# First projection after each of the last three norms, issued as two 128-token halves

## The chip, the cores and the metric

The kernel runs on one NeuronCore of a Trainium2 chip. The metric is device time in microseconds (us) of one execution, as a median over runs.

## What is computed

256 tokens of width 1024 go through two model blocks. The change touches only the second block, whose reference, cut down, is:

```python
def second_block(x, mem, ...):
    z = rmsnorm(h, mix_norm_g) @ w_in                 # h: 256 tokens x 1024
    y = concatenate([pool(z), rwkv7(z), diff_attention(z)])
    h = h + y @ w_out
    h = h + memory_cross_attention(rmsnorm(h, xa_norm_g), rmsnorm(mem, mem_norm_g),
                                   xa_wq, xa_wk, xa_wv, xa_wo, ...)
    h = h + conv_ffn(rmsnorm(h, ffn_norm_g), ffn_w_up, ffn_conv_w, ffn_conv_b, ffn_w_down)
    return h
```

So three norms stand ahead of three projections: the layer norm that ends the first model block (it feeds `w_in`), the norm ahead of `xa_wq`, and the norm ahead of `ffn_w_up`. All inputs are float32.

## The kernel before

**Split products.** Every large product is made of three: a float32 operand is split into `hi` (rounded, type fp32r) and `lo` (the rest), and hi·hi, lo·hi and hi·lo are summed in PSUM. `split` (line 198) does it with one ScalarE activation and one VectorE subtraction. Weights arrive as blocks of 128 x 1024 floats: `ws` loads one with a DMA into `raw` (3 buffers) and splits it into `hi` and `lo` (4 buffers each).

**Projections with the tokens in the free dimension.** `gemm_f` (line 225) multiplies one weight block (128 output features) with the activations `xh`, `xl`, which lie as 8 tiles of 128 features x 256 tokens. That is 3 x 8 = 24 matmuls, each with its own 128 x 128 stationary piece of the weights and 256 moving columns. Two such blocks, 48 matmuls, fill one PSUM tile `mm` of 128 x 512 floats. Pool `pm` has two `mm` tiles, used in turn.

**Output projections.** `rows_gemm` (lines 237 and 262) computes tokens x 1024 outputs into four accumulators: two token halves `tb`, each with two column halves. Its last 3 weight blocks (`TAIL`) are kept back and used for all of `tb=0` first, then for `tb=1`, so that the norm of the first 128 tokens can begin while the second half is still being multiplied.

**The norm in halves.** `done(tb)` runs for each half. For two of the three norms it is `add_turn`: VectorE adds the residual (line 474) and multiplies with the norm's gain (475); `turn` transposes four 128 x 128 pieces on TensorE into PSUM (line 280, tile `tp`), and `put` splits them to `xh`, `xl` (198). The per-token scale is not waited for: `row_norm` (ScalarE, 350) works out the mean square, and the scale is multiplied in behind the projection. For the layer norm of the first block, `layer_norm` (lines 399 to 438) does the same with more VectorE steps.

**Work that fills the layer norms.** Behind three layer norms, `rows_gemm` takes a `Fill`: 48 matmuls of the memory keys (line 94, tile `mk`) that are pinned in the order 30, 8, 10 around the transposes of `tb=1`:

```python
FILL = 30, 8, 10
...
            if fill is not None and tb == 1:
                self.turned, self.tgate = [], fill.part(FILL[0], ins)
            if done is not None:
                done(tb)
        if fill is not None:
            fill.rest()
```

`tgate` pins the transposes behind the first part; `turned` holds the last transpose of each column half, behind which the parts of 8 and 10 go; `pgate` pins the next projection behind the last transpose. These pins set only the order on TensorE. The rest of the order on each engine is settled by a scheduler before the program is compiled; each engine then runs its list strictly in order.

**The three places.** In this text place 1 is `columns` in `mixer` (weights `mix_f`, behind the layer norm with its `Fill` of memory keys), place 2 is `cross` (weights `xa_wq`, behind `add_turn`, without a fill), and place 3 is `ffn` (weights `ffn_up`, behind `add_turn`, without a fill).

Of the kernel before, what the change touches and what calls it, by code (L numbers as in the profile page):

```python
# [38 lines left out]
FILL = 30, 8, 10  # L39
# [6 lines left out]
class Parts:  # L46


    def __init__(self, parts):
        self.parts = parts  # L50
# [8 lines left out]
class Fill:  # L59
# [12 lines left out]
    def before(self, k):  # L72
        for f, i in self.at.get(k, ()):
            f(i)
# [32 lines left out]
    def rest(self):  # L107
        K, nc, h = self.K, self.K.nc, self.h
        self.part(FILL[1], K.turned[0])
        self.part(FILL[2], K.turned[1])  # L110
        p = self.p
        sq, k = (K.t2(n).rearrange("p (a b) -> p a b", a=2) for n in ("xsq", "mkey"))
        nc.scalar.activation(sq, p, AF.Square)
        for a in range(2):
            nc.scalar.activation(k[:, a], p[:, a], AF.Copy, scale=K.v("xk", a))

        def owed():
            nc.vector.tensor_add(sq[:, 0], sq[:, 0], sq[:, 1])
            ss = K.big("xss")
            for tb in range(2):  # L120
                nc.tensor.matmul(ss[:, tb:tb + 1], sq[:, 0, tb * 128:(tb + 1) * 128], K.ones[:, 0:1], start=True, stop=True)
            r = K.small(4, "kr")
            nc.vector.tensor_scalar(r[:, 2:4], ss[:, 0:2], 1.0 / 256, RMS_EPS, op0=OP.mult, op1=OP.add)
            K.power(r[:, 0:2], r[:, 2:4], 2)
            r = K.row_scale(r)
            nc.vector.tensor_mul(k, k, r[:, None, :].to_broadcast([128, 2, 256]))
            nc.sync.dma_start(K.kd[:, h], k.rearrange("p a b -> p (a b)"))

        K.owed = owed


class Kern:
# [992 lines left out]
    def mixer(self):  # L1125
        I = self.I
        xh, xl = self.xh, self.xl
        zp = self.page("zp")
        z = zp[:, 0:2048].rearrange("p (c t) -> p c t", c=8)

        A, T = self.page("rwA"), self.page("rwT")
        self.mk = self.load(A[:, 2560:3712].rearrange("p (m t) -> p m t", m=9), I["masks"])
        self.load(T[:, 2816:3328], I["lora"])
        self.load(T[:, 3584:4096].rearrange("p (c t) -> p c t", c=2), I["invcount"])
        self.rb = zp[:, 3840:4096]
        self.columns(z, 0, xh, xl)
        ypg = self.pages.tile([128, 2, 8, 256], F32R, name="ypg", tag="pg")
        yh, yl = (Parts([ypg[:, i, 0:4], ypg[:, i, 4:8]]) for i in range(2))
        self.weave((self.rwkv(z, A, T, yh, yl), 0, 0.8), (self.others(zp, A, T, xh, xl, yh, yl), 0, 1), (self.memory_kv(), MEM0, 0.8))
        accs = self.accs()  # L1140
        order = [4, 5, 6, 7, 0, 1, 2, 3]
        self.rows_gemm(accs, 8, lambda i: I["mix_out"][order[i]], lambda i: (yh, yl, order[i]), self.add_turn(accs, 1))

    def columns(self, dst, c0, xh, xl):
        for c in range(0, dst.shape[1], 2):
            p = self.mm().rearrange("p (a b) -> p a b", a=2)
            for a in range(2):
                hi, lo = self.ws(self.I["mix_f"][c0 + c + a], 1024)
                self.gemm_f(p[:, a, :], hi, lo, xh, xl, 8)
            if c0 + c < 4:  # L1150

                self.nc.scalar.activation(dst[:, c:c + 2], p, AF.Copy)
                if c == 2:
                    self.nc.scalar.activation(self.rb, self.row_scale(self.rn[:, 2:4]), AF.Copy)
                    for i in range(0, 4, 2):
                        self.nc.vector.tensor_mul(dst[:, i:i + 2], dst[:, i:i + 2], self.rb[:, None, :].to_broadcast([128, 2, 256]))
                    self.pay()
            else:
                self.nc.vector.tensor_mul(dst[:, c:c + 2], p, self.rb[:, None, :].to_broadcast([128, 2, 256]))
# [391 lines left out]
    def cross(self):  # L1551
        nc, I = self.nc, self.I
        kT, vt = self.mem
        xh, xl = self.xh, self.xl
        qp = self.page("qp")
        q = qp[:, 0:2048].rearrange("p (h a m) -> p h a m", h=4, a=2)
        PTs = qp[:, 2048:4096].rearrange("p (h k q) -> p h k q", h=4, k=2)
        norm = self.small(18, "xnorm")
        nc.vector.tensor_scalar(norm[:, 16:18], self.rn[:, 0:2], RMS_EPS, None, op0=OP.mult)
        for h in range(4):  # L1560
            p = self.mm().rearrange("p (a b) -> p a b", a=2)
            for a in range(2):
                hi, lo = self.ws(I["xa_wq"][h * 2 + a], 1024)
                self.gemm_f(p[:, a, :], hi, lo, xh, xl, 8)
            sq = self.t2("xsq").rearrange("p (a b) -> p a b", a=2)
            nc.scalar.activation(sq, p, AF.Square)
            for a in range(2):
                nc.scalar.activation(q[:, h, a], p[:, a], AF.Copy, scale=self.v("xq", a))
            nc.vector.tensor_add(sq[:, 0], sq[:, 0], sq[:, 1])
            ss = self.big("xss")  # L1570
            for tb in range(2):
                nc.tensor.matmul(ss[:, tb:tb + 1], sq[:, 0, tb * 128:(tb + 1) * 128], self.ones[:, 0:1], start=True, stop=True)
            r = norm[:, 2 * h:2 * h + 2]
            nc.vector.scalar_tensor_tensor(norm[:, 8 + 2 * h:10 + 2 * h], ss[:, 0:2], 1.0 / 256, norm[:, 16:18], op0=OP.mult, op1=OP.add)
            self.power(r, norm[:, 8 + 2 * h:10 + 2 * h], 2)
            nc.vector.tensor_scalar(r, r, 1.0 / 16, None, op0=OP.mult)
        opg = self.pages.tile([128, 2, 8, 256], F32R, name="xopg", tag="pg")
        oh, ol = (Parts([opg[:, i, 0:4], opg[:, i, 4:8]]) for i in range(2))
        for h in range(4):
            p = self.mm("s").rearrange("p (a b) -> p a b", a=2)  # L1580
            for tb in range(2):
                for a in range(2):
                    nc.tensor.matmul(p[:, tb], q[:, h, a, tb * 128:(tb + 1) * 128], kT[:, h, a], start=a == 0, stop=a == 1)
            self.softmax_t(p, norm[:, 2 * h:2 * h + 2], PTs[:, h])
            o = self.acc("o").rearrange("p (a b) -> p a b", a=2)
            for a in range(2):
                for mb in range(2):
                    c = h * 256 + a * 128
                    nc.tensor.matmul(o[:, a], vt[:, mb, c:c + 128], PTs[:, h, mb], start=mb == 0, stop=mb == 1)  # L1589
            self.split(oh.two(2 * h), ol.two(2 * h), o)  # L1590
        accs = self.accs()
        self.rows_gemm(accs, 8, lambda k: I["xa_wo"][k], lambda k: (oh, ol, k), self.add_turn(accs, 2))


    def ffn(self):
        nc, I = self.nc, self.I
        xh, xl = self.xh, self.xl
        w = I["ffn_up"]
        zs = []
        accs = None  # L1600
        gp = []
        for i in range(22):
            p = self.mm().rearrange("p (a b) -> p a b", a=2)
            for a in range(2):
                hi, lo = self.ws(w[a * 22 + i], 1024)
                self.gemm_f(p[:, a, :], hi, lo, xh, xl, 8)
            if i == 0:
                self.nc.scalar.activation(self.rb, self.row_scale(self.rn[:, 2:4]), AF.Copy)
            q = self.t2("q").rearrange("p (a b) -> p a b", a=2)
            nc.vector.tensor_mul(q, p, self.rb[:, None, :].to_broadcast([128, 2, 256]))  # L1610
            p = q
            c = self.t1("conv")
            cw = lambda j: self.v("cw", i * 3 + j)
            nc.scalar.activation(c, p[:, 0], AF.Identity, scale=cw(2), bias=self.v("cb", i))
            nc.vector.scalar_tensor_tensor(c[:, 1:], p[:, 0, :255], cw(1), c[:, 1:], op0=OP.mult, op1=OP.add)
            nc.vector.scalar_tensor_tensor(c[:, 2:], p[:, 0, :254], cw(0), c[:, 2:], op0=OP.mult, op1=OP.add)
            nc.scalar.activation(c, c, AF.Gelu)
            nc.vector.tensor_mul(c, c, p[:, 1])
            if i % 8 == 0:
                pg = self.pages.tile([128, 2, 8, 256], F32R, name="zf%d" % i, tag="pg")  # L1620
                gp.append([[pg[:, j, 0:4], pg[:, j, 4:8]] for j in range(2)])
            zh, zl = (Parts(gp[-1][j]) for j in range(2))
            self.split(zh[i % 8], zl[i % 8], c)
        zh, zl = (Parts([x for g in gp for x in g[j]]) for j in range(2))
        accs = self.accs()
# [168 lines left out]
```

## Time and profile before

| what | value |
|---|---|
| median of 3 runs | 2427.48 us (2427.36 to 2429.73) |
| the profiled execution: its own time | 2427.72 us |
| the profiled execution: span from first to last instruction | 2425.9 us |
| TensorE (PE) busy with matmuls | 2386.3 us, 98% of the span |
| TensorE busy with weight loads (PEld) | 2187.8 us, 90% |
| VectorE (DVE) busy | 1730.5 us, 71% |
| ScalarE (ACT) busy | 1185.7 us, 49% |
| GpSimd (POOL) busy | 50.9 us, 2% |
| mean granted TensorE clock, as a share of full speed | 0.996 |

TensorE's instructions overlap, so the busy time of one matmul is longer than the step from one to the next; the step is the start of the next row less the start of this one, over the number of matmuls. Idle time is shown in square brackets with the instruction that ended it.

### The profile page before, as it was taken

Reading aid. Unit: us, or ns where it says so; the run is one execution under the profiler, and the core shown is the slowest. Engines: PE = TensorE matmul, PEld = TensorE weight load, DVE = VectorE, ACT = ScalarE, POOL = GpSimd, SP = SyncE. Lnnn points to the kernel's source line nnn. Section 1 sums busy time; section 2 is a strip of 40 time slices with the busy share of each in tenths; the row PEclk is TensorE's granted clock in tenths of the full one; section 3 lists DMA queues with packets and bytes.
Section 4 is the critical chain, followed back from the end, with each engine's and each line's share of the span. In section 5 each row is a group of like instructions: output and inputs, shape, how many; then the busy total and the mean of one; then the engine's idle time right before and its main releaser. Section 6 shows DMA issues by size and latency. Waiting matters only on the chain.

```text
span 2425.9 us, 40782 instructions
## 1 busy us (share of the span) xinstructions
PE 2386.3 (98%) x16184; PEld 2187.8 (90%) x16184; DVE 1730.5 (71%) x3197; ACT 1185.7 (49%) x1620; POOL 50.9 (2%) x62
## 2 busy tenths in 40 slices
PE   8999999999999999989999999999999998999999
PEld 8888999999988888888999999998888887888997
DVE  8576699888755555676599888855555678765884
ACT  5454555444454444455555444444444455434553
POOL 0000000000000000000000000000000011000000
PEclk9999999999999999999999999999999999999999
DMA  6555554444555666634645444455666755133654
GB/s 229 186 210 203 192 185 174 154 160 158 173 190 192 217 205 220 204 116 158 222 168 189 158 156 159 165 185 192 196 227 200 248 168 167 62 110 122 195 183 156
DMA packets 121247, 433.82 MB, mean 179 GB/s; under 512 B 13920, under 2 KB 14560, under 8 KB 119648
## 3 DMA queue, kind: packets, MB, share of 16 engines
q1 hardware_dynamic: 120336, 430.95, 52.7%
q8 instruction: 127, 2.08, 0.3%
q14 instruction: 64, 0.52, 0.1%
q10 hardware_dynamic: 720, 0.26, 0.0%
HBM read 424.61 MB, written 6.55 MB: 178 GB/s over the span
## 4 chain that ended last, share of the span: by engine, by line
PE 95%; DVE 2%; ACT 1%; DMA 1%; issue 1%; POOL 0%; ACTq 0%; DVEq 0%
PE mm L225 45%; PE acc L237 37%; PE G L840 3%; PE acc L262 2%; PE mk L94 1%; PE scp L760 1%; PE y L670 1%; PE kq L225 1%; PE tp L280 1%; DVE lo L198 0%; PE c L225 0%; PE pXT L1453 0%; PE pX L1449 0%; ACT hi L198 0%; PE o L1589 0%
## 5 line engine op out<-in xcount | busy, mean ns | idle before, releaser
L198 DVE TENSOR_TENSOR lo<-raw,hi 128x1024 fp32r<-128x1024 f32 x752 | 917.0, 1223 | 462.3 <-ACT hi L198 460.5
L198 ACT ACTIVATE hi<-raw 128x1024 fp32r<-128x1024 f32 x752 | 791.4, 1056 | 757.0 <-PE acc L237 313.5
L225 PE MATMUL mm<-xh,hi 128*128 128x256 f32 x3056 | 445.8, 287 | 13.0 <-ACT hi L198 7.9
L225 PE MATMUL mm<-xl,hi 128*128 128x256 f32 x3056 | 436.1, 284 | 0.0
L225 PE MATMUL mm<-xh,lo 128*128 128x256 f32 x3056 | 433.0, 284 | 0.0
L225 PEld LDWEIGHTS mm<-xh,hi 128*128 128x128 f32 x3056 | 397.0, 192 | 15.7 <-ACT hi L198 7.9
L225 PEld LDWEIGHTS mm<-xl,hi 128*128 128x128 f32 x3056 | 396.9, 193 | 0.5 <-issue 0.5
L225 PEld LDWEIGHTS mm<-xh,lo 128*128 128x128 f32 x3056 | 396.0, 193 | 0.0
L237 PE MATMUL acc<-lo,xh 128*128 128x512 f32 x1112 | 345.4, 390 | 0.0
L237 PE MATMUL acc<-hi,xh 128*128 128x512 f32 x1112 | 344.9, 390 | 0.0
L237 PE MATMUL acc<-hi,xl 128*128 128x512 f32 x1112 | 344.5, 389 | 0.0
L237 PEld LDWEIGHTS acc<-hi,xl 128*128 128x128 f32 x1112 | 209.0, 188 | 43.6
L237 PEld LDWEIGHTS acc<-lo,xh 128*128 128x128 f32 x1112 | 209.2, 188 | 43.3
L237 PEld LDWEIGHTS acc<-hi,xh 128*128 128x128 f32 x1112 | 209.0, 188 | 43.3 <-issue 0.3
L819 ACT ACTIVATE H<-mm 128x512 f32<-128x512 f32 (+30 forms) x118 | 55.2, 468 | 193.2 <-PE mm L225 193.0
L198 DVE TENSOR_TENSOR xl<-H,xh 128x1024 fp32r<-128x1024 f32 x64 | 78.2, 1225 | 48.3 <-ACT xh L198 48.3
L198 ACT ACTIVATE xh<-H 128x1024 fp32r<-128x1024 f32 x64 | 67.5, 1058 | 57.5 <-PE acc L237 56.7
L840 PE MATMUL G<-h 128*128 128x128 f16 x1024 | 78.3, 220 | 0.0
L834 DVE TENSOR_TENSOR h<-iota,idxT 128x512 f16<-128x512 f16 x128 | 53.7, 421 | 26.8 <-PE G L840 26.6
L851 DVE SCALAR_TENSOR_TENSOR H<-G,H 128x512 f32<-128x512 f32 (+26 forms) x110 | 60.3, 551 | 13.8 <-ACT H L819 13.4
L840 PEld LDWEIGHTS <-h 128*128 128x128 f16 x1024 | 59.0, 97 | 4.8
L837 DVE TENSOR_TENSOR h<-h,idxT 128x512 f16<-128x512 f16 x128 | 53.6, 420 | 0.0
(519 smaller groups left out, 2150.8 us busy)
## 6 DMA issues: line engine op xcount, KB each, us to landing
raw<-in_peer_u_dram SPq DMA_DIRECT2D x256, 512.0 KB, 3.3
raw<-in_peer_v_dram SPq DMA_DIRECT2D x256, 512.0 KB, 4.2
raw<-in_ffn_up_dram SPq DMA_DIRECT2D x44, 512.0 KB, 3.6
raw<-in_peer_q_dram SPq DMA_DIRECT2D x32, 512.0 KB, 4.3
raw<-in_ffn_down_dram SPq DMA_DIRECT2D x22, 512.0 KB, 3.5
raw<-in_ret_g_dram SPq DMA_DIRECT2D x16, 512.0 KB, 4.0
raw<-in_ret_qk_dram SPq DMA_DIRECT2D x16, 512.0 KB, 3.7
raw<-in_ret_v_dram SPq DMA_DIRECT2D x16, 512.0 KB, 4.4
```

Source lines behind the costliest of these rows:

```text
L94: yield nc.tensor.matmul(self.p[:, a, :], self.W[:, 2 * a + w, k * 128:(k + 1) * 128], self.X[:, k, x], start=k == 0 and j == 0, stop=k == ...
L198: return self.nc.scalar.activation(hi, src, AF.Copy), self.nc.vector.tensor_sub(lo, src, hi.bitcast(F32))
L225: ins = self.nc.tensor.matmul(out, l[:, k * m:(k + 1) * m], r[k], start=k == 0 and j == 0, stop=k == nk - 1 and j == 2)
L237: ins = self.nc.tensor.matmul(o, l, r[:, c * n:(c + 1) * n], start=first and j == 0, stop=last and j == 2)
L262: last, ins = ins, self.nc.tensor.matmul(o, l[k][:, ts], r[:, c * 512:(c + 1) * 512], start=nk <= TAIL and i == 0 and j == 0, stop=i == le ...
L280: return self.nc.tensor.transpose(out, in_, self.ident)
L670: nc.tensor.matmul(y, AT[:, h, m, n * 128:(n + 1) * 128], vt[:, m, h * 512:(h + 1) * 512], start=m == 0, stop=m == 1)
L819: nc.scalar.activation(dst[:, :, tok:], p[:, :, tok:], AF.Gelu)
L834: nc.vector.tensor_tensor(o1, io, val[0], op=OP.is_equal)
L837: nc.vector.tensor_mul(o2, o2, val[2])
L840: nc.tensor.matmul(G[:, 4 * k + t, :], o1[:, t // 2, :, t % 2], o[:, t // 2, :, t % 2], start=i == 0, stop=i == 1)
L851: nc.vector.scalar_tensor_tensor(H[:, :n, ts], Gi[:, 64 * i:64 * i + n], 1 / GS, H[:, :n, ts], op0=OP.mult, op1=OP.mult)
```

## The change

A new class `Early` issues the first two weight blocks behind each of the three norms as half products: for each block 24 matmuls over the first 128 tokens, and after both blocks are done for those tokens, the same over the other 128. At places 2 and 3 it is given to `rows_gemm` as its `fill`: 30 half products stand ahead of the transposes of `tb=1`, and 18 more behind them (the 8 pinned behind the first column half, the 10 behind the second); the 48 of the second token half follow. At place 1, where the `Fill` of memory keys stays, all 96 come behind the transposes.

```diff
+class Early:
+    def __init__(self, K, w):
+        self.K, self.w = K, w
+        self.todo = None
+    def before(self, k):
+        pass
+    def products(self):
+        K = self.K
+        self.p = K.mm("early").rearrange("p (a b) -> p a b", a=2)
+        blocks = [K.ws(w, 1024) for w in self.w]
+        for tb in range(2):
+            ts = slice(tb * 128, (tb + 1) * 128)
+            for a, (hi, lo) in enumerate(blocks):
+                for j, (l, x) in enumerate(((hi, K.xh), (lo, K.xh), (hi, K.xl))):
+                    for k in range(8):
+                        yield K.nc.tensor.matmul(self.p[:, a, ts], l[:, k * 128:(k + 1) * 128], x[k][:, ts],
+                                                 start=k == 0 and j == 0, stop=k == 7 and j == 2)
+    def part(self, n, first):
+        if self.todo is None:
+            self.todo = self.products()
+        for i in range(n):
+            self.K.last = next(self.todo)
+            if i == 0:
+                self.K.after(self.K.last, first)
+        return self.K.last
+    def rest(self):
+        self.part(FILL[1], self.K.turned[0])
+        self.part(FILL[2], self.K.turned[1])
+        self.K.pgate = None
+    def all(self):
+        if self.todo is None:
+            self.part(48, self.K.turned[1])
+            self.K.pgate = None
+        for self.K.last in self.todo:
+            pass
+        return self.p
...
-        self.rows_gemm(accs, 8, lambda i: I["mix_out"][order[i]], lambda i: (yh, yl, order[i]), self.add_turn(accs, 1))
+        self.early = Early(self, I["xa_wq"][0:2])
+        self.rows_gemm(accs, 8, lambda i: I["mix_out"][order[i]], lambda i: (yh, yl, order[i]), self.add_turn(accs, 1), fill=self.early)
...
-            p = self.mm().rearrange("p (a b) -> p a b", a=2)
-            for a in range(2):
-                hi, lo = self.ws(self.I["mix_f"][c0 + c + a], 1024)
-                self.gemm_f(p[:, a, :], hi, lo, xh, xl, 8)
+            if c0 + c == 0:
+                p = Early(self, self.I["mix_f"][0:2]).all()
+            else:
+                p = self.mm().rearrange("p (a b) -> p a b", a=2)
+                for a in range(2):
+                    hi, lo = self.ws(self.I["mix_f"][c0 + c + a], 1024)
+                    self.gemm_f(p[:, a, :], hi, lo, xh, xl, 8)
...
-        self.rows_gemm(accs, 8, lambda k: I["xa_wo"][k], lambda k: (oh, ol, k), self.add_turn(accs, 2))
+        self.early = Early(self, (I["ffn_up"][0], I["ffn_up"][22]))
+        self.rows_gemm(accs, 8, lambda k: I["xa_wo"][k], lambda k: (oh, ol, k), self.add_turn(accs, 2), fill=self.early)
```

In `cross` (for `h == 0`) and `ffn` (for `i == 0`) the two `gemm_f` calls give way to `p = self.early.all()` in the same way. The changed file is 47 lines longer ahead of these functions, so line 280 of before is 327 after, 198 is 245, 225 is 272, 262 is 309, 350 is 397 and 361 is 408; the half products are line 151.

At place 3, TensorE's list before, from the last product of the output projection (`acc`) over the transposes (`tp`) to the projection (`mm`; `rb` carries the per-token scale):

```order
L262 MATMUL acc<-hi,xopg 128x512
L280 MATMUL tp<-ident,rms 128x128 x16
L225 MATMUL mm<-xh,hi 128x256 x8
L225 MATMUL mm<-xh,lo 128x256 x8
L225 MATMUL mm<-xl,hi 128x256 x4
L361 MATMUL rb<-ident,R 128x128
L225 MATMUL mm<-xl,hi 128x256 x4
```

The same place on the same engine in the changed kernel:

```order
L309 MATMUL acc<-hi,xopg 128x512
L327 MATMUL tp<-ident,rms 128x128 x8
L151 MATMUL early<-xh,hi 128x128 x8
L151 MATMUL early<-xh,lo 128x128 x8
L151 MATMUL early<-xl,hi 128x128 x8
L151 MATMUL early<-xh,hi 128x128 x6
L327 MATMUL tp<-ident,rms 128x128 x8
L151 MATMUL early<-xh,hi 128x128 x2
L408 MATMUL rb<-ident,R 128x128
L151 MATMUL early<-xh,lo 128x128 x8
L151 MATMUL early<-xl,hi 128x128 x8
```

The 16 transposes are now 8 and 8 with 30 half products between them; in all 96 matmuls of 128 columns take the place of 48 of 256. Place 2 has the same list, with one `acc` product still between the first two groups of four transposes.

ScalarE at place 3 before (`xh<-tp` copies a transposed half, `rms,ss<-h` is the mean square, `hi<-raw` splits a weight block):

```order
L198 ACTIVATE hi<-raw 128x1024 x5
L198 ACTIVATE xh<-tp 128x4x128 x2
L350 ACTIVATE rms,ss<-h 128x1024
L198 ACTIVATE xh<-tp 128x4x128 x2
L350 ACTIVATE rms,ss<-h 128x1024
L198 ACTIVATE hi<-raw 128x1024 x3
```

And after:

```order
L245 ACTIVATE hi<-raw 128x1024 x5
L245 ACTIVATE xh<-tp 128x4x128 x2
L397 ACTIVATE rms,ss<-h 128x1024
L245 ACTIVATE hi<-raw 128x1024 x2
L245 ACTIVATE xh<-tp 128x4x128 x2
L397 ACTIVATE rms,ss<-h 128x1024
L245 ACTIVATE hi<-raw 128x1024 x3
```

Two weight splits moved ahead of the copies of the second token half; VectorE's `lo` steps moved with them.

At place 1, TensorE's list before, with what each instruction waits for (a name is the engine whose semaphore is waited on):

```order
L94 MATMUL mk<-fill 128x256 x10
L225 MATMUL mm<-xh,hi 128x256 [waits DVE_49]
L225 MATMUL mm<-xh,hi 128x256 x3
L225 MATMUL mm<-xh,hi 128x256 [waits Activation_49]
L225 MATMUL mm<-xh,hi 128x256 x3
```

And after:

```order
L94 MATMUL mk<-fill 128x256 x10
L151 MATMUL early<-xh,hi 128x128 [waits DVE_49]
L151 MATMUL early<-xh,hi 128x128 x3
L151 MATMUL early<-xh,hi 128x128 [waits Activation_49]
L151 MATMUL early<-xh,hi 128x128 x3
```

Nothing moved here: the first half product stands where the first full product stood and also waits for VectorE.

## Rows read from the trace of the kernel before

**Rows 1.** The page: the chain that ended last, share of the span by engine.

```profile
PE 95%; DVE 2%; ACT 1%; DMA 1%; issue 1%; POOL 0%; ACTq 0%; DVEq 0%
```

**Rows 2.** Chain that ended last, in order: start us, us, what it ran.

```profile
1964.44 13.26 PE mm L225 x96
...
2237.60 0.22 PE rb L361 x2
...
2239.48 122.88 PE mm L225 x1024
2362.36 51.71 PE acc L237 x228
```

**Rows 3.** Timeline, place 2: start us, us, instruction, shapes, [idle before <-releaser].

```profile
2163.50 0.60 PE L280 MATMUL tp<-ident,rms 128*128 128x128 f32 x4
...
2164.13 1.27 ACT L198 ACTIVATE xh<-tp 128x512 fp32r<-128x512 f32 x2 [6.84 <-PE tp L280]
...
2164.17 1.04 PE L280 MATMUL tp<-ident,rms 128*128 128x128 f32 x8
...
2166.31 0.66 PE L280 MATMUL tp<-ident,rms 128*128 128x128 f32 x4 [1.11 <-DVE rms L475]
...
2166.97 1.42 PE L225 MATMUL mm<-xh,hi 128*128 128x256 f32 x8
...
2168.23 1.11 PE L225 MATMUL mm<-xh,lo 128*128 128x256 f32 x8
```

**Rows 4.** Timeline, place 3.

```profile
2231.64 1.47 PE L280 MATMUL tp<-ident,rms 128*128 128x128 f32 x12
...
2232.28 1.09 ACT L198 ACTIVATE xh<-tp 128x512 fp32r<-128x512 f32 x2 [6.13 <-PE tp L280]
...
2234.94 1.23 PE L225 MATMUL mm<-xh,hi 128*128 128x256 f32 x8 [0.97 <-ACT xh L198]
...
2236.00 1.12 PE L225 MATMUL mm<-xh,lo 128*128 128x256 f32 x8
...
2236.28 1.07 ACT L198 ACTIVATE hi<-raw 128x1024 fp32r<-128x1024 f32 x1
```

**Rows 5.** Timeline, place 1.

```profile
1957.63 1.18 ACT L198 ACTIVATE xh<-u 128x512 fp32r<-128x512 f32 x2
...
1963.70 0.69 DVE L198 TENSOR_TENSOR xl<-tp,xh 128x512 fp32r<-128x512 f32 x1
...
1964.44 1.27 PE L225 MATMUL mm<-xh,hi 128*128 128x256 f32 x8 [2.40 <-DVE xl L198]
```

**Rows 6.** Windows: stretch, its us, busy per engine, then granted PE clock, DMA share, GB/s.

```profile
1965.50:1968.90 3.40, 3.40 (x18) 3.40 (x17) 3.40 (x5) 0.04 (x1) 0.00 (x0) 0.50 0.51 164
...
2163.50:2167.00 3.50, 2.38 (x19) 1.84 (x17) 2.60 (x6) 2.72 (x5) 0.01 (x1) 1.00 0.00 0
...
2231.60:2235.00 3.40, 2.23 (x18) 1.72 (x16) 2.79 (x6) 2.72 (x6) 0.27 (x1) 1.00 0.00 0
```

**Rows 7.** Timeline of weight loads (PEld) around matmuls of one column, place 2.

```profile
2179.14 0.54 PEld L1572 LDWEIGHTS xss<-ones,xsq 128*128 128x128 f32 x4
2179.59 0.42 PEld L225 LDWEIGHTS mm<-xh,hi 128*128 128x128 f32 x3
```

**Rows 8.** Timeline, matmuls of 64 and 128 columns with float32 weights.

```profile
2043.04 1.97 PE L1405 MATMUL pv<-ident,W 128*128 128x64 f32 x16 [1.05 <-DVE W L1400]
2044.85 2.00 PE L1410 MATMUL pm<-rwab 128*128 128x128 f32 x16
```

**Rows 9.** Timeline, matmuls of 128 columns with float16 weights.

```profile
407.41 1.08 PE L840 MATMUL G<-h 128*128 128x128 f16 x16
408.30 0.84 PE L225 MATMUL mm<-xh,hi 128*128 128x256 f32 x5
```

**Rows 10.** Tiles: durations of weight loads in ns (min/median/max), first and last start.

```profile
L225 PEld LDWEIGHTS mm<-xh,hi x3056: 186/192/333, 7.9 to 2360.0; 128*128 128x128 f32 x191
...
L1405 PEld LDWEIGHTS pv<-ident,W x16: 186/192/192, 2043.0 to 2044.7; 128*128 128x128 f32 x16
```

More of the change, by code (lines that the diff above doesn't have):

```diff
@@ L1560, in cross @@
         for h in range(4):
[L1561 to L1564, printed above, removed]
+            if h == 0:
+                p = self.early.all()
+            else:
+                p = self.mm().rearrange("p (a b) -> p a b", a=2)
+                for a in range(2):
+                    hi, lo = self.ws(I["xa_wq"][h * 2 + a], 1024)
+                    self.gemm_f(p[:, a, :], hi, lo, xh, xl, 8)
             sq = self.t2("xsq").rearrange("p (a b) -> p a b", a=2)
@@ L1602, in ffn @@
         for i in range(22):
[L1603 to L1606, printed above, removed]
+            if i == 0:
+                p = self.early.all()
+            else:
+                p = self.mm().rearrange("p (a b) -> p a b", a=2)
+                for a in range(2):
+                    hi, lo = self.ws(w[a * 22 + i], 1024)
+                    self.gemm_f(p[:, a, :], hi, lo, xh, xl, 8)
             if i == 0:
```

## The prediction, made before the changed kernel was run

> **What bounds the kernel now.** I read the page first. The chain that ended last runs on TensorE for 95% of the span [rows 1], so whatever lengthens TensorE's list lengthens the run, unless it fills a wait. The chain in order of time then shows how fast that list runs: 1024 products of 256 columns in 122.88 us, or 0.120 us each, and 228 products of 512 columns in 51.71 us, or 0.2268 us each [rows 2]. Last I read the timelines of the three places for what TensorE waits for.
>
> At place 2 the transposes start at 2163.50 and the projection's second group of 8 starts at 2168.23 [rows 3]. In these 4.73 us stand 16 transposes, one product of 512 columns and 8 products of 256. A transpose takes 0.11 us (eight take 1.04 and four 0.60 [rows 3]), so 1.76 + 0.23 + 0.96 = 2.95 us is work and 1.78 us is waiting. At place 3 the same stretch is 2236.00 - 2231.64 = 4.36 us [rows 4], less 1.76 + 0.96: 1.64 us of waiting. In both, TensorE waits for VectorE to make the second token half and for ScalarE to copy it. At place 1 it waits 2.40 us for a VectorE step, `xl<-tp` [rows 5], and then runs 3.4 us at a granted clock of 0.50, the 1.2 GHz level [rows 6].
>
> **What the change removes.** At places 2 and 3 the first half products need only the first 128 tokens. At place 3 eight transposes end at 2231.64 + 0.88 = 2232.52; ScalarE's two copies run from 2232.28 for 1.09 us [rows 4], so the first is done at about 2232.82 and the second at 2233.37. Half products 1 to 4 read the first and wait 0.33 us; 5 to 8 wait 0.10 us more. The second token half's transposes then stand 30 half products later, when their inputs have long been ready. So 0.43 us of waiting stays of 1.64: 1.21 us is gained. At place 2 the same working, with transposes done at 2163.50 + 0.88 + 0.23 = 2164.61 and copies from 2164.13 for 1.27 us [rows 3], leaves 0.37 of 1.78: 1.41 us is gained.
>
> At place 1 I count no gain. The copies `xh` of the first 128 tokens begin at 1957.63 and take 1.18 us [rows 5], so these tokens were there long before TensorE stopped waiting at 1964.44. The wait is for a buffer: the new tile `early` comes from the same pool of two `mm` tiles as before, one of them holds the transposes that the VectorE step at 1963.70 reads, the other the memory keys. The order shows the same wait on VectorE at the first half product.
>
> **What it adds.** At each place 48 products of 256 columns (48 x 0.120 = 5.76 us) become 96 of 128 columns. Arithmetic does not grow, but the number of weight loads doubles, since every half product loads its own 128 x 128 stationary piece. No row shows an fp32r product of 128 columns, so its step is bounded. From below: 256 columns fewer save 0.2268 - 0.120 = 0.107 us [rows 2], so 128 fewer save 0.053 and a half product would take 0.067 us if the load stayed hidden. From above, with nothing saved, 0.120 us.
>
> The nearest rows speak for the upper end. Four matmuls of a single column each, with float32 weights, start their loads at 2179.14, and the load after them starts at 2179.59 [rows 7]: 0.1125 us per load with next to no columns to stream. Sixteen of 64 columns take 2044.85 - 2043.04 = 1.81 us, 0.113 us each [rows 8]. These are two-pass float32 products, but the load itself is alike: 192 ns median for `W` and 192 ns for the fp32r `hi` [rows 10]. So a load of 128 x 128 four-byte weights can follow another only after 0.11 us; under 256 columns (0.120) it is just hidden, under 128 it is the bound. Against this stand the float16 products of 128 columns: 16 from 407.41 to 408.30, 0.0556 us each [rows 9]. Their weights have two bytes, so I take the four-byte rows: 0.112 us.
>
> The Trainium skill, "TensorE: Matmul & The Clock Gate", has rules on either side. Its "Back-to-back issue gap" gives columns/2.4 + 2.5 ns, which is 56 ns here and fits the float16 rows; its "LDWEIGHTS" gives 128/1.2 = 107 ns for a load, and "Weight-path perf modes" says that fast loading does not hold for FP32, which fits the one-column rows. By the first rule a place would cost 96 x 0.056 - 5.76 = -0.4 us, by the second about +4.5 us.
>
> With 0.112, a place costs 96 x 0.112 - 5.76 = 10.75 - 5.76 = +4.99 us. This lies on TensorE's own list, with nothing beside it to hide it.
>
> **What is moved.** ScalarE does two weight splits of 1.07 us [rows 4] ahead of the second half's copies, which puts these back by some 2.1 us. They have cover: the transposes that these copies read come 30 half products (3.4 us) later than the first ones, and 18 more (2.0 us) stand between them and the first product that needs the copies. Without it the two splits would show as up to 2.1 us at either place. The blocks' buffers come free later, the first after 72 half products, the second after 96; two more blocks are split by then, 5.76 us of work for TensorE, against a split that takes 1.07 us on ScalarE and a like step on VectorE. At place 1 the load of the eighth `mix_f` block goes behind nine small loads in SP's queue; five blocks of 2.88 us lie between the freeing of its buffer and its use, so I cost it at nothing. The `rb` products (0.22 us each [rows 2]) stay as they are.
>
> **The sum.** 3 x 4.99 - 1.21 - 1.41 = +12.35 us. The profiled execution took 2427.72 us, 0.24 above the median of the three runs and inside their spread. 2427.72 + 12.35 = 2440.1; I say 2440.0 us, 0.5% slower. A measurement of this kernel can tell about 0.2%, 4.9 us, from no change.
>
> **Rivals.**
> - *Columns set the step after all.* fp32r loads hide as the float16 ones do. For it: rows 9, and that a load overlaps the matmul ahead. Against it: rows 7 and 8. At 0.056 us: 3 x (5.38 - 5.76) - 2.62 = -3.8 us, 2424; at 0.067 us: 3 x 0.67 - 2.62 = -0.6 us, 2427. This is the case on the other side: the change breaks even where 3 x (96p - 5.76) = 2.62, at p = 0.069 us, and is slower by over 0.2% from 0.086 us. The Trainium skill's same section also gives 81 ns for sustained pairs of load and matmul of 128 columns; that would be +3.4 us, 2431. Chance of this case 0.10.
> - *The clock falls too.* Half products leave the array idle for half of the time, and after a 2.40 us wait at place 1 the granted clock fell to 0.50 for 3.4 us [rows 5, 6]. At places 2 and 3, where TensorE is busy 2.38 of 3.50 and 2.23 of 3.40 us, it stayed at 1.00 [rows 6]. The change shortens these waits, which speaks against it. One such fall at half rate costs 1.7 us: at both places 2443.5, and more if it lasts through all half products. Chance 0.05.
> - *The narrow product leaves the fast form.* A true float32 product of 128 columns takes 0.22 us (`rb` [rows 2]). If 128 columns of fp32r ran so, a place costs 96 x 0.22 - 5.76 = 15.4 us, in all 2471. Nothing in the trace speaks for it. Chance 0.05.
> - *Place 1 gains as well*, if its wait is for the second token half and not for the tile: up to 2.40 us less, 2437.7. The order speaks against it. It lies inside the forecast's own range.
>
> **How the numbers follow.** The forecast (step near 0.11 us) has 0.80. Its own range: with 0.120 us and one fall of the clock, 3 x 5.76 - 2.62 + 1.7 = +16.4, 2444; with half of place 1's cost taken up later by waits of VectorE and the remaining waits gone too (0.8 us), 12.35 - 2.5 - 0.8 = +9.0, 2437. Down to 2434 it takes in steps around 0.09 us between the cases. So 2434 to 2445. Faster by over 0.2% needs a step under 0.053 us: 0.02. Within 0.2%: the rest of the first rival, 0.08. Slower: 0.90.
>
> **What would show it.** Right: rows of `early` with 8 matmuls starting every 0.9 us and loads every 0.11; at place 3 the first half products near 2232.9, at place 1 still near 1964.4 and behind `xl`; each place's 96 over some 10.8 us; no idle ahead of the second transposes. Wrong: groups of 8 every 0.45 to 0.55 us (the first rival), every 1.7 us (the third), a granted clock of 0.50 at place 2 or 3, or ScalarE's moved splits ending a wait of TensorE.

## The result and the profile after

| kernel | median (range), runs | ratio to before, 95% interval |
|---|---|---|
| before | 2427.42 us (2425.99 to 2429.73), 6 runs | |
| changed | 2451.79 us (2448.96 to 2452.83), 6 runs | 1.0095 (1.0085 to 1.0105) |

The change costs 24.4 us, about twice the 12.35 us forecast; 2451.8 lies above the range of 2434 to 2445. The profiled execution spans 2450.6 us, 24.7 more than before. It is one of four executions at 2451.2 to 2452.8 us with a mean granted clock of 0.991; the other two took 2449.0 and 2449.7 at 0.993.

The page of the changed kernel, first its busy time by engine, then the chain that ended last (in rows 1 PE had 95%):

```profile
PE 2413.3 (98%) x16328; PEld 2214.3 (90%) x16328; DVE 1731.6 (71%) x3197; ACT 1185.9 (48%) x1620; POOL 51.9 (2%) x62
...
PE 96%; DVE 2%; ACT 1%; DMA 1%; issue 1%; POOL 0%; ACTq 0%; DVEq 0%
```

TensorE is busy 27 us longer, and the engines other than TensorE hardly changed. So the question is where on TensorE's list the time went. The timeline of PE at place 1 answers to [rows 5]:

```profile
1963.94 1.25 PE L151 MATMUL early<-xh,hi 128*128 128x128 f32 x8 [2.42 <-DVE xl L245]
1964.98 1.91 PE L151 MATMUL early<-xh,lo 128*128 128x128 f32 x8
1966.69 1.91 PE L151 MATMUL early<-xl,hi 128*128 128x128 f32 x8
...
1983.76 2.02 PE L272 MATMUL mm<-xh,hi 128*128 128x256 f32 x8
...
1988.84 1.11 PE L272 MATMUL mm<-xh,hi 128*128 128x256 f32 x8
...
1991.71 0.61 PE L408 MATMUL rb<-ident,R 128*128 128x128 f32 x4
```

The wait for `xl` is the same as before (2.42 against 2.40 us), as forecast. But from the second group on, eight half products take 1.71 us, 0.2135 us each and not 0.112, and the first full-width products behind them are slow as well. Only from 1988.84 do eight full-width products take 0.95 us. The windows (stretch, its us, busy per engine, granted clock, DMA share, GB/s) say why; they answer to [rows 6]:

```profile
1965.20:1989.00 23.80, 23.80 (x114) 23.80 (x115) 8.93 (x12) 4.79 (x7) 3.26 (x5) 0.51 0.48 154
...
2040.30:2047.00 6.70, 6.17 (x17) 5.07 (x18) 6.19 (x15) 2.71 (x6) 3.60 (x2) 0.52 0.43 131
2060.80:2064.10 3.30, 3.30 (x17) 3.24 (x16) 1.47 (x5) 1.21 (x4) 0.00 (x0) 0.55 0.76 215
2183.00:2197.00 14.00, 14.00 (x126) 14.00 (x126) 8.09 (x13) 8.99 (x15) 1.10 (x2) 1.00 0.45 150
2251.50:2266.00 14.50, 14.25 (x122) 13.76 (x122) 9.79 (x15) 8.14 (x12) 1.12 (x2) 1.00 0.34 110
```

For 23.8 us TensorE is busy without a gap and the granted clock is 0.51, the 1.2 GHz level. Before, the same wait cost 3.4 us at 0.50 [rows 6]. At places 2 and 3 (the last two lines) the clock stays at 1.00. The chain in order of time gives the size of each piece:

```profile
1963.94 20.02 PE early L151 x96
...
2041.92 7.79 PE acc L284 x24
...
2060.29 3.38 PE pm L1461 x16
```

The rows of the kernel before that these and the next readings are compared with, first from its timeline of PE, then from its chain (`acc`, `pm` and further on `pv` and `pM` are tiles of the stages behind place 1; the tile `pm` is not the pool `pm`):

```profile
1977.54 0.61 PE L361 MATMUL rb<-ident,R 128*128 128x128 f32 x4
...
2173.98 1.12 PE L225 MATMUL mm<-xh,lo 128*128 128x256 f32 x8
...
2242.20 1.12 PE L225 MATMUL mm<-xh,lo 128*128 128x256 f32 x8
...
2027.75 6.74 PE acc L237 x24
...
2045.01 1.85 PE pm L1410 x16
```

- **Place 1.** From the first product to the first `rb` it took 1991.71 - 1963.94 = 27.77 us; before, 1977.54 - 1964.44 = 13.10. That is +14.67 where +4.99 stood.
- **Behind place 1**, the 24 `acc` products took 7.79 us (6.74 in the chain before) and the 16 `pm` 3.38 (1.85): +1.05 and +1.53, in the windows with clocks of 0.52 and 0.55. Before, the clock was at 0.50 from 2023.50 to 2030.30, over the first of these `acc` products too, and at 1.00 over `pm`.
- **Places 2 and 3**, from the first transpose to the second group of the third block:

```profile
2180.55 0.60 PE L327 MATMUL tp<-ident,rms 128*128 128x128 f32 x4
...
2183.01 1.06 PE L151 MATMUL early<-xh,lo 128*128 128x128 f32 x8
2183.90 1.06 PE L151 MATMUL early<-xl,hi 128*128 128x128 f32 x8
...
2194.68 1.12 PE L272 MATMUL mm<-xh,lo 128*128 128x256 f32 x8
...
2252.46 1.03 PE L327 MATMUL tp<-ident,rms 128*128 128x128 f32 x8
2253.74 1.15 PE L151 MATMUL early<-xh,hi 128*128 128x128 f32 x8 [0.25 <-ACT xh L245]
...
2257.19 1.06 PE L327 MATMUL tp<-ident,rms 128*128 128x128 f32 x8
...
2266.85 1.12 PE L272 MATMUL mm<-xh,lo 128*128 128x256 f32 x8
```

Place 2: 14.13 us against 10.48 before (2163.50 to 2173.98), +3.65; forecast 4.99 - 1.41 = 3.58. Place 3: 14.39 against 10.56 (2231.64 to 2242.20), +3.83; forecast 3.78. Eight half products take 0.89 us, 0.111 to 0.112 each. The second token half's transposes (2257.19) wait for nothing, and ScalarE's moved splits end no wait of TensorE. The five terms add up to 14.67 + 1.05 + 1.53 + 3.65 + 3.83 = 24.73 us, and the spans differ by 24.7. That the two agree to the last digit is chance: the changed kernel begins place 1 0.50 us earlier (1963.94 against 1964.44), so about 0.5 us more lies in small pieces outside the five terms.

### The profile page after: what moved, and what is told of

Same layout as the page of the kernel before. It is cut to its first block, busy times and chain, and to the rows that moved or that the text cites. A ratio compares the mean times of both kernels' runs of the same rounds, so it can differ in the third digit from the quotient of the medians.

```text
span 2450.6 us, 41070 instructions
## 1 busy us (share of the span) xinstructions
PE 2413.3 (98%) x16328; PEld 2214.3 (90%) x16328; DVE 1731.6 (71%) x3197; ACT 1185.9 (48%) x1620; POOL 51.9 (2%) x62
## 4 chain that ended last, share of the span: by engine, by line
PE 96%; DVE 2%; ACT 1%; DMA 1%; issue 1%; POOL 0%; ACTq 0%; DVEq 0%
PE mm L272 44%; PE acc L284 37%; PE G L887 2%; PE acc L309 2%; PE early L151 2%; PE mk L94 1%; PE scp L807 1%; PE tp L327 1%; PE y L717 1%; PE kq L272 1%; DVE lo L245 0%; PE c L272 0%; PE pXT L1504 0%; PE pX L1500 0%; PE o L1643 0%
## 5 line engine op out<-in xcount | busy, mean ns | idle before, releaser
L272 PE MATMUL mm<-xh,hi 128*128 128x256 f32 x3008 | 439.7, 287 | 9.1 <-ACT hi L245 7.8
L272 PE MATMUL mm<-xl,hi 128*128 128x256 f32 x3008 | 429.0, 284 | 0.0
L272 PE MATMUL mm<-xh,lo 128*128 128x256 f32 x3008 | 426.5, 284 | 0.0
L272 PEld LDWEIGHTS mm<-xh,hi 128*128 128x128 f32 x3008 | 391.5, 192 | 11.1 <-ACT hi L245 7.8
L272 PEld LDWEIGHTS mm<-xl,hi 128*128 128x128 f32 x3008 | 390.5, 193 | 0.5 <-issue 0.5
L272 PEld LDWEIGHTS mm<-xh,lo 128*128 128x128 f32 x3008 | 389.9, 193 | 0.0
```

The source lines that it names most:

```text
L272: ins = self.nc.tensor.matmul(out, l[:, k * m:(k + 1) * m], r[k], start=k == 0 and j == 0, stop=k == nk - 1 and j == 2)
```

## The experiments

Theory: two separate things cost time, the load-bound step of 0.112 us at all three places, and at place 1 a granted clock that falls behind the wait and does not come back while half products run. Rivals: the half products are slow at place 1 for another reason (their loads, their buffers, their number), or the places disturb each other. Differences are to the runs of the kernel before on the same chip: 2428.05 us (19 runs) for the first four kernels, 2427.93 (24 runs) for the next four and 2427.34 (21 runs) for the last three.

**1. Places 2 and 3 alone.** Against the changed kernel:

```diff
-            if c0 + c == 0:
-                p = Early(self, self.I["mix_f"][0:2]).all()
-            else:
...
+            p = self.mm().rearrange("p (a b) -> p a b", a=2)
```

> Half products at places 2 and 3 alone; place 1 as before. Theory (places 2 and 3 cost what was predicted, the surplus is place 1's clock): 96 half products a place at 0.112 us each, waits mostly gone, +3.65 and +3.83 us, so about +7.5 us, 2435, with a granted clock of 1.00 at both places. Rival (the half products cost more than was predicted everywhere): +12 us or more.

Measured 2435.41 us, ratio 1.0028 (1.0018 to 1.0037): +7.4, as expected. The terms of places 2 and 3 were right.

**2. Place 1 alone.** `fill=self.early` and the calls in `cross` and `ffn` taken back.

> Half products at place 1 alone. Theory (TensorE starts them at a granted clock of 0.50 after the 2.40 us wait and, as long as only half products run, the clock is not given back): some 23 us at 0.5, +14.7 us at the place, and up to 2.5 us more from falls of the clock further on, 2442 to 2445. Rival (the surplus comes from places 2 and 3 or from their sum): +5 us, 2432.

Measured 2444.50 us, ratio 1.0062 (1.0045 to 1.0078): +16.4, with a granted clock of 0.50 over 23.7 us:

```profile
1966.30:1990.00 23.70, 23.70 (x112) 23.70 (x112) 9.05 (x12) 4.79 (x7) 3.26 (x5) 0.50 0.48 153
```

With experiment 1 it makes 23.8 of the 24.4 us, so within their spread the places add up and do not disturb each other.

**3. The whole change, without the wait at place 1.** The last 24 products of the memory keys are issued once more into the same tile (their values don't change), and TensorE does them in place of waiting (`h == 3` is the `Fill` at place 1):

```diff
+        if h == 3:
+            for j, (w, x) in enumerate(((0, 0), (1, 0), (0, 1))):
+                for k in range(8):
+                    ins = nc.tensor.matmul(self.p[:, 1, :], self.W[:, 2 + w, k * 128:(k + 1) * 128], self.X[:, k, x],
+                                           start=k == 0 and j == 0, stop=k == 7 and j == 2)
+            K.pgate = K.turned[1] = ins
```

> The whole change, and 24 of the memory-key products of 256 columns are done once more (same operands, same result) in the wait of place 1, so that TensorE does not stand still for 2.40 us there. Theory: the clock stays at 1.00 through the half products, place 1 costs 0.5 us for what sticks out of the repeated products and 10.75 + 5.76 - 13.26 = 3.3 us, in all some +11 us, 2438. Rival (half products pull the clock down by themselves at this place): 0.5 again, +24 us or more, 2452.

Measured 2439.28 us, ratio 1.0042 (1.0026 to 1.0059): +11.2, where the changed kernel has +24.4, with 24 matmuls more. The window over its half products at place 1:

```profile
1964.60:1975.20 10.60, 10.60 (x97) 10.60 (x97) 8.04 (x12) 4.58 (x8) 3.17 (x5) 1.00 0.59 192
```

The same 96 half products, with the same operands, take 0.89 us per eight once no standstill is ahead of them. So without the wait the clock stays up at this place, and with the clock up the forecast's step holds.

**4. The same 24 products in the kernel before.**

> The kernel before with the same 24 repeated products in the wait of place 1. Theory: the 3.4 us at a granted clock of 0.50 behind this wait go away; they cost 1.7 us, the repeated products stick out by 0.5 us, so -1.2 us, 2426. Rival (the clock falls for another reason than the wait): +0.5 to +2.9 us.

Measured 2428.58 us, ratio 1.0001 (0.9991 to 1.0010): the expected gain of 1.2 us did not show, though the interval does not rule it out. Three windows of the profiled execution, at place 1 and at two falls of the clock further on (the first of them is in the kernel before as well):

```profile
1961.30:1975.70 14.40, 14.40 (x123) 14.40 (x122) 12.10 (x18) 9.40 (x14) 2.00 (x4) 1.00 0.49 166
2022.80:2029.50 6.70, 4.60 (x13) 3.83 (x14) 6.63 (x16) 2.31 (x5) 2.09 (x1) 0.51 0.63 157
2043.30:2050.00 6.70, 6.70 (x30) 6.34 (x30) 4.25 (x8) 1.61 (x3) 0.00 (x0) 0.51 0.77 212
```

The clock stayed up at place 1 and `rb` came 1.84 us earlier (1975.70 against 1977.54), but in this execution (2429.65 us) the clock fell over `pm` at 2043.30, where before it was at 1.00, and `pM` behind it is 1.46 us late (2048.15 against 2046.69). This is one of three executions at a mean granted clock of 0.996; the seven at 0.997 have a median of 2427.96 us, no clear gain either. So that fall is hardly the whole reason, and what else takes the gain is open.

**5. The same number of loads at place 1, at full width.** Place 1 alone again; both passes multiply all 256 tokens, so the 48 products are done twice:

```diff
-            ts = slice(tb * 128, (tb + 1) * 128)
+            ts = slice(0, 256)
```

> Place 1 alone with the same 96 products and 96 weight loads, but each over all 256 columns (everything is computed twice, the second time over the first). Theory (products of full width bring the clock back, half products do not): the clock is at 0.50 for 3.4 us as before, then 1.00, and 48 more products of 0.120 us cost +5.8 us, 2433, less than the half products with half the columns. Rival (it is the number of weight loads at this place): some 23 us at 0.50, +16 us, 2444.

Measured 2434.50 us, ratio 1.0027 (1.0016 to 1.0038): +6.6, where experiment 2 has +16.4, for twice the columns.

```profile
1965.40:1968.70 3.30, 3.30 (x18) 3.30 (x18) 3.30 (x5) 0.00 (x0) 0.00 (x0) 0.52 0.70 176
1968.90:1983.00 14.10, 14.10 (x120) 14.10 (x119) 6.39 (x9) 5.92 (x9) 3.26 (x5) 1.00 0.71 239
```

After 3.3 us the clock is back, as in [rows 6]. What the edit changes between the two kernels is the columns of each product alone, so the number of loads, the buffers and the order of the blocks are out as causes.

**6. Product series by themselves.** Ahead of `ffn`'s last stage, five series of fp32r products into a tile of their own (`dm`): 200 of 128 columns, 48 with 64 weight columns, 48 of 64, 48 of 192 and 48 of 256 columns.

> The kernel before with five series of fp32r matmuls ahead of the last projection (they compute nothing that is used): 200 with 128 x 128 weights and 128 columns, then 48 each with 128 x 64 weights and 128 columns, with 128 x 128 weights and 64, 192 and 256 columns. Theory (the load of four-byte weights sets the step): 0.112 us at 64, 128 and 192 columns alike, 0.120 at 256, and about 0.06 to 0.07 at 128 columns with half the weights; the clock stays at 1.00 through the 22 us of the first series. Rival (columns set it): 0.04, 0.067, 0.093 and 0.120 us, and the half weights change nothing.

One execution: 2471.59 us. The windows, for these matmuls alone (PE and PEld busy, then clock, DMA share, GB/s):

```profile
2362.00:2382.00 20.00, 20.00 (x181) 20.00 (x181) 1.00 0.06 24
2383.50:2386.10 2.60, 2.60 (x47) 2.60 (x45) 1.00 0.03 6
2386.40:2390.30 3.90, 3.90 (x38) 3.90 (x36) 1.00 0.00 0
2390.60:2392.40 1.80, 1.80 (x10) 1.80 (x10) 0.50 0.00 0
2397.40:2400.00 2.60, 2.60 (x25) 2.60 (x25) 1.00 0.00 0
2400.40:2405.80 5.40, 5.40 (x48) 5.40 (x47) 1.00 0.01 3
```

20.00 / 181 = 0.1105 us at 128 columns; with half as wide a stationary piece 2.60 / 47 = 0.055 us; 0.103 at 64 columns, 0.104 at 192, 0.1125 at 256 (a matmul cut by a window's edge counts whole, so the values of the short windows are some per cent low). The step follows the weight load and not the moving columns, up to 192 of them at least. And the clock: it stayed at 1.00 through 20 us of 128-column products, but fell to 0.50 at 2390.4, by the count of products inside the series of 64 columns, with TensorE busy all the time; it was back at 1.00 at 2397.4, within the series of 192 columns. The 2.6 us ahead of the 64-column series were the products with half as wide weights, so which of the two series brought the fall is not separated.

**7. A shorter wait at place 1, in the kernel before.** VectorE's step on the second 128 tokens that is needed only later (line 437; line 438 needs its result) is pinned behind the split of a weight block (`first`), which stands behind the copies, so that `xl` comes earlier:

```diff
-                    nc.vector.scalar_tensor_tensor(y[:, 1], y[:, 1], m, gb[:, 0], op0=OP.subtract, op1=OP.mult)
+                    a = nc.vector.scalar_tensor_tensor(y[:, 1], y[:, 1], m, gb[:, 0], op0=OP.subtract, op1=OP.mult)
+                    if first is not None:
+                        self.after(a, first)
```

> The kernel before, with the two VectorE steps of the last layer norm that are needed later (lines 437 and 438, 1.28 us each) pinned behind the copies that place 1 waits for. Theory: the wait of 2.40 us shrinks to some 0.5 us, and if it is short enough the clock does not fall: -1.9 us, or -3.5 us with the clock, 2424 to 2426. Rival (other work is late next, the split of the first weight block or the norm's scale): no change, or up to +2 us.

Measured 2428.49 us, ratio 0.9998 (0.9989 to 1.0007): no gain. The timeline shows the wait for `xl` down from 2.40 to 0.22 us and eight products in 0.96 us from the second group on, but two new waits for the norm's scale:

```profile
1962.62 1.21 PE L225 MATMUL mm<-xh,hi 128*128 128x256 f32 x8 [0.22 <-DVE xl L198]
...
1976.40 0.49 PE L361 MATMUL rb<-ident,R 128*128 128x128 f32 x2 [2.01 <-DVE R L360]
...
1977.09 1.20 PE L225 MATMUL mm<-xh,hi 128*128 128x256 f32 x8
1978.13 1.12 PE L225 MATMUL mm<-xh,lo 128*128 128x256 f32 x8
...
1982.38 0.68 PE L361 MATMUL rb<-ident,R 128*128 128x128 f32 x4 [1.24 <-DVE R L360]
```

The clock did not fall behind the wait of 2.01 us: the eight products from 1977.09 took 1.04 us. So a wait of about this length is not always followed by a fall.

**8. One block in halves, not two, at places 2 and 3.** 16 half products ahead of the second token half's transposes, 32 behind them; the second block in full width.

> Places 2 and 3 only, and there only the first block (24 products) in halves, 16 of them ahead of the transposes of the second token half; the second block in full width. Theory (a product that is split costs 2 x 0.112 - 0.120 = 0.104 us, and the filled waits give back 1.2 and 1.4 us): 48 x 0.104 - 2.6 = +2.4 us, 2430. Rival (the waits are worth more than the loads cost once fewer products are split): below the kernel before.

Measured 2431.36 us, ratio 1.0012 (1.0003 to 1.0022): +3.4, one more than expected and about half of experiment 1. A product split in two costs 2 x 0.112 - 0.120 = 0.104 us more, and the half that goes ahead fills at most 0.112 us of waiting. So a split wins next to nothing even where the half fills a wait, and here some of the halves fill none; splitting less only loses less.

**9. Experiment 7 with the scale applied one pair of blocks later.**

```diff
-            if c0 + c < 4:
+            if c0 + c < 6:
...
-                if c == 2:
+                if c == 4:
...
-                    for i in range(0, 4, 2):
+                    for i in range(0, 6, 2):
```

> The kernel before with VectorE's steps on the low halves pinned behind the copies, and the row scale rb of the first projection applied one pair of blocks later. Theory: the two rb waits of 2.01 and 1.24 us that ate the gain of the pinned copies are now behind work that TensorE has anyway, while the 2.4 us wait at place 1 stays gone and the clock stays at 1.00: 2 to 3.5 us less than the kernel before, 2424.5 to 2426. Rival: the first rb broadcast still comes too early for VectorE, or VectorE's work on what follows the projection starts later by what the scale was moved: no change, or up to 3 us more.

Measured 2429.56 us, ratio 1.0005 (0.9996 to 1.0014): no change, as the rival had it. The first `rb` still comes behind the fourth block, and waits; in the profiled execution the clock, at 1.00 through the first 96 products, falls there:

```profile
1977.42 0.49 PE L361 MATMUL rb<-ident,R 128*128 128x128 f32 x2 [1.82 <-DVE R L360]
...
1978.20:1981.60 3.40, 3.40 (x18) 3.40 (x18) 2.72 (x5) 0.56 (x1) 3.40 (x3) 0.51 1.00 389
```

Here a wait of 1.82 us for the same instruction is followed by a fall, where the 2.01 us of experiment 7 were not. Why, no run settles.

**10 and 11. The same products at place 1 in two orders.** Place 1 alone; one of the two blocks goes in halves, either the second or the first:

```diff
-        for tb in range(2):
-            ts = slice(tb * 128, (tb + 1) * 128)
-            for a, (hi, lo) in enumerate(blocks):
+        for a, ts in ((0, slice(0, 256)), (1, slice(0, 128)), (1, slice(128, 256))):   # experiment 10
+        for a, ts in ((0, slice(0, 128)), (0, slice(128, 256)), (1, slice(0, 256))):   # experiment 11
+            for hi, lo in (blocks[a],):
```

> Only place 1 changed: its first block in full width (24 products of 256 columns), then its second block in two halves (48 products of 128 columns). Theory (the clock that the wait takes away comes back behind full-width products, and half-width ones neither bring it back nor let it fall): granted clock 0.50 for about 3.4 us, then 1.00, with half products at 0.112 us; 48 x 0.112 - 24 x 0.120 = 2.5 us more than before, 2430.5. Rival (half products hold the clock down wherever they stand, or only the number of loads and columns counts): 0.50 again in the second block, and a time within 1 us of the kernel with the order reversed.

> The same operands, loads and columns at place 1 in the other order: the first block in two halves (48 products of 128 columns), then the second in full width (24 products of 256). Theory: granted clock 0.50 through the 48 half products (0.2135 us each, 10.2 us) and some 3.4 us of full-width ones, then 1.00; 48 x 0.2135 - 24 x 0.120 - what the wait's slow full products cost before (1.4 us is saved later, since the slow stretch of full products stands anyway) = 6.6 to 10 us more than before, 2434.5 to 2438, so 4 us or more above the kernel with full width first. Rival (order does not matter): equal times, about 2430.5 or both about 2436.

The timeline of PE with full width first (these files are one line shorter, so the half products are line 150):

```profile
1964.84 1.61 PE L150 MATMUL early<-xh,hi 128*128 128x256 f32 x8 [2.41 <-DVE xl L244]
1966.25 1.91 PE L150 MATMUL early<-xh,lo 128*128 128x256 f32 x8
...
1969.31 1.00 PE L150 MATMUL early<-xh,hi 128*128 128x128 f32 x8
1970.15 1.06 PE L150 MATMUL early<-xh,lo 128*128 128x128 f32 x8
1971.04 1.06 PE L150 MATMUL early<-xl,hi 128*128 128x128 f32 x8
...
1980.41 0.61 PE L407 MATMUL rb<-ident,R 128*128 128x128 f32 x4
```

And with halves first:

```profile
1963.89 1.36 PE L150 MATMUL early<-xh,hi 128*128 128x128 f32 x8 [2.41 <-DVE xl L244]
1965.05 1.91 PE L150 MATMUL early<-xh,lo 128*128 128x128 f32 x8
...
1973.59 2.02 PE L150 MATMUL early<-xh,hi 128*128 128x256 f32 x8
...
1978.57 1.12 PE L271 MATMUL mm<-xh,hi 128*128 128x256 f32 x8
...
1984.33 0.61 PE L407 MATMUL rb<-ident,R 128*128 128x128 f32 x4
```

Behind full-width products the halves run at 0.111 us (0.89 per eight); ahead of them at 0.2135 from the second group on, and the full-width ones behind are slow as well until 1978.57, 4.98 us after the first of them. To the first `rb` (at 1980.41 and 1984.33) it takes 15.57 and 20.44 us: +2.47 and +7.34 over the 13.10 of before, as the theory gave it (2.5; 6.6 to 10). The whole times are 2434.69 (ratio 1.0026, 1.0017 to 1.0035) and 2437.76 us (1.0040, 1.0025 to 1.0056): the order costs 3.1 us, where the theory asked for 4 or more. The missing part lies behind place 1. In experiment 10's profile the clock fell once more over `pv` and `pm` (at 2048 to 2054, `pM` +7.8 us by then), as in experiment 4; in experiment 11's it did not. Experiment 10's ten times range from 2431.20 to 2436.34 us, four of them below 2432.1, near the 2430.5 expected; the profiled one took 2435.04.

No version here beats the kernel before.

## Why the prediction was wrong

- **The step of a half product** (0.112 us, the load as the bound) was right: 0.112 at places 2 and 3, 0.1105 by itself. The rival that columns set the step is dead, and so is a narrow product that leaves the fast form: experiment 6 has 128 columns at half its 0.22 us.
- **Slips in its working.** The rows give 0.40 and 0.34 us of waiting left at places 3 and 2 where 0.43 and 0.37 stand, and its formula gives a step of 0.052 us where 0.053 stands for a gain of over 0.2%. They change nothing.
- **The gains at places 2 and 3** (1.41 and 1.21 us) were right to 0.1 us, and so was the cover of ScalarE's moved splits.
- **No gain at place 1** was right: the first half product waits 2.42 us for the same `xl`. That it is the tile's buffer which waits was argued from the order, and only fits; no run gave `early` another tile.
- **The step that failed** is the sum's line 3 x 4.99. It took places 1 to 3 as alike and priced place 1 at the full clock, though [rows 6] showed the clock at 0.50 right where the half products would stand. Place 1 measured +14.67, not +4.99. The mechanism was among the rivals ("The clock falls too", and "more if it lasts through all half products"), but it was looked for at places 2 and 3, where nothing fell. Eleven of the twelve groups at 0.2135 us instead of 0.112 are 88 x 0.1015 = 8.9 of the 9.7 us that were missing. The rows could show that the half products would begin at the low clock; that it would last through all of them, and not for the 3.4 us of before, was in no row and came out of the runs.
- **Left out altogether**: what a shift does to later falls of the clock, +1.05 and +1.53 us here. The fall over `acc` was there before and took longer; the one over `pm` is new, and experiments 4 and 10 show such a fall there too. Why one execution has it and another not is open; no run settled it.

The cause at place 1 is shown by these runs: without the standstill the halves run fast (3), with full-width products behind the same standstill the clock comes back (5, 10), with halves behind it, it does not until they are over (2, 11). What makes a fall follow one wait and not another is not shown: the waits of 2.01 us (7) and 1.82 us (9) ahead of the same `rb` came out differently.

The Trainium skill, "TensorE: Matmul & The Clock Gate", section "What's actually happening", lets the clock follow how busy TensorE has lately been. The fall after the wait agrees (2.42 us idle, then 0.51). The rise does not, if busy is what the profile calls busy: here the engine was busy for the whole 23.8 us, 88 half products in a row among them, and the clock stayed at 0.51. The measurement decides.

## What to carry to other kernels

Before narrowing matmuls, look at the granted clock where they will stand, and price each place at its own clock: the same edit cost 3.7 to 3.8 us where the clock was up and 14.7 where it had fallen behind a wait. If narrow products must follow a wait, put wide ones first (+2.47 against +7.34 us at place 1 here). With the four-byte weights of this kernel, halving the moving columns from 256 to 128 saves next to nothing per matmul (0.120 to 0.112 us) and doubles their number, so it wins next to nothing even where every half that goes ahead fills a wait.

## What the hardware showed that was not expected

- TensorE can be busy without a gap and still not get its clock back: 23.8 us at 0.51 on 128-column fp32r products, while the same products held 1.00 for 20 us when the clock was up (experiment 6).
- The clock can fall with no standstill at all: in experiment 6 it went to 0.50 at 2390.4 us within 64-column fp32r products, which stood behind products with half as wide weights. The 64-column step is nearly that of 128 columns (0.103 against 0.1105 us).
- A wait does not settle it either: behind 2.01 us of waiting the clock stayed at its upper level (experiment 7), behind 1.82 us at the same instruction it fell to 0.51 (experiment 9).
- A kernel with 24 more matmuls was 13 us faster (experiment 3 against the changed kernel, +11.2 against +24.4), and one with twice the columns at place 1 10 us faster (experiment 5 against 2, +6.6 against +16.4).
